# Two-layer hybrid trunk on one core: where raw weight blocks, W_down sums and the norm's ones-matmul stand

## The chip, the cores and the metric

The kernel runs on one core of a Trainium2 chip. The metric is the device time of one execution in microseconds; of several runs the median counts.

## The reference

The model is a trunk of two layers on an input of 1024 tokens by 1024 features, all in float32. Layer 0 mixes sparse attention with a Mamba-2 block, layer 1 is a short gated convolution, and behind each comes a SwiGLU network with a hidden width of 2816. The change touches what follows the attention:

```
def _short_conv_layer(x, norm_w, in_w, conv_w, out_w):
    h = _rmsnorm(x, norm_w) @ in_w
    gate_b, gate_c, v = _split(h, (SC_WIDTH, SC_WIDTH, SC_WIDTH))
    y = gate_b * _causal_dwconv(gate_c * v, conv_w)
    return x + y @ out_w

def _swiglu_ffn(x, norm_w, w_gate, w_up, w_down):
    h = _rmsnorm(x, norm_w)
    return x + (jax.nn.silu(h @ w_gate) * (h @ w_up)) @ w_down
```

The order is attention, FFN of layer 0 (here FFN0), short convolution (conv), FFN of layer 1 (FFN1), final norm.

## The kernel before

**Stages.** FFN0, conv and FFN1 are built alike. A stage normalises its input, multiplies it with the weights of the in-projection, combines the results elementwise, spills operands to DRAM, and then runs the out-projection (`out_products`). FFN0's and FFN1's in-projections have 22 units each, 11 pairs of a gate and an up block of 256 columns; conv's has 12, in 4 groups of c, v and b.

**A unit.** Every matrix product is made by a Strassen-Winograd scheme with 7 block products instead of 8. Each float32 operand is split into a high and a low part (`split`: ScalarE casts the high part, L176, VectorE subtracts it, L177), so a product of 4 blocks is 12 matmuls of 512 columns (`prod`, L1275 to L1277), and a full unit has 84. A unit's raw weights come as a pair of 512 KB tiles named `wr` (L1222). VectorE makes four sums of their quarters (L1198, L1201, tiles `s` and `wr`) and each block is split into a tile `wc`.

**Early products.** The norm of the two halves of the tokens isn't ready at the same time. Products 1 and 2 need the first half alone, so they are made ahead for the first 6 units of a stage (`early`). Their raw blocks (128x4x128, 256 KB, 12 in a stage) are loaded by `early_steps` (L1251) into the same two `wr` buffers that the pairs use; the pair tiles for the first unit come behind them. `norm_second` (L1492) normalises the second half: one matmul with a matrix of ones (L996) adds up the squares over the partitions, ScalarE takes the inverse root (L1004, L1005), VectorE multiplies (`scalar_tensor_tensor`, 8 of them, shown below as x<-x,c,sq). Before the change, it is called ahead of the first early product. In FFN1 it also holds `turn`, which transposes the residual on TensorE (L173) and stores it.

**W_down sums.** The out-projection's weights need sums of blocks too. They are made while the in-projection runs (`wsums`): for each of 11 pairs (4 groups in conv) four 256 KB loads into tiles `wd` (L1350, 4 buffers shared with other x tiles), four additions or subtractions, and four stores into a scratch tensor `d_wl` (L1340). In the kernel before, GpSimd (POOL) issues the loads and the stores and does the arithmetic. The out-projection then reads the sums back (L1389, tiles `lr`).

**What sets the order.** The program is written in one order, and a scheduler with a simulated timeline orders the instructions of each engine from it; buffers are handed out round robin by tag: `wr` has 2, `w` (the split weights) 8, `x` 4, `s` 32 and `t`, for temporaries, 42. A list of steps (`Steps`) makes the weights of a product 7 products ahead. SP's queue carries the weight loads, reads of operands, and stores of operands (`keep`, L1340 on SP).

Of the kernel before, what the change touches and what calls it, by code (L numbers as in the profile page):

```python
# [8 lines left out]
F32 = mybir.dt.float32  # L9
# [8 lines left out]
P = 128  # L18
# [3 lines left out]
HF = 512  # L22
# [81 lines left out]
class Trunk:  # L104
# [1108 lines left out]
    def unit_steps(self, src, prods, parts):  # L1213

        nc = self.nc
        st = {}

        def begin():
            st["r"] = []
            for i in range(2):  # L1220
                r = self.wp.tile([P, 4, 256], F32, name=self.uid("wr"), tag="wr", bufs=2)
                nc.sync.dma_start(r, src[i * HF:(i + 1) * HF].rearrange("(k p) m -> p k m", p=P))  # L1222
                st["r"].append(r)

        def step(i):
            if "r" not in st:
                begin()
            r0, r1 = st["r"]
            a11, a21, a12, a22 = r0[:, :, :P], r0[:, :, P:], r1[:, :, :P], r1[:, :, P:]
            if i == 6:  # L1230
                s3 = self.s(nm="s3")
                st["s3"] = s3.rearrange("p (k m) -> p k m", k=4)
                self.sub(st["s3"], a11, a21)
                self.add(a21, a21, a22)
                self.sub(a11, a21, a11)
            if i == 3:
                self.sub(a12, a12, a11)
            return self.wsplit({1: a11, 2: a12, 3: a12, 4: a22, 5: a21, 6: a11, 7: st.get("s3")}[i], 4)

        for i in prods:  # L1240
            if i in parts:
                self.st.note(parts[i])
            self.st.add(lambda i=i: step(i))

    def early_steps(self, src):

        nc = self.nc

        def step(i):
            r = self.wp.tile([P, 4, P], F32, name=self.uid("wr"), tag="wr", bufs=2)  # L1250
            nc.sync.dma_start(r, src[i * HF:(i + 1) * HF, :P].rearrange("(k p) m -> p k m", p=P))  # L1251
            return self.wsplit(r, 4)

        for i in range(2):
            self.st.add(lambda i=i: step(i))
# [31 lines left out]
        self.add(t, self.prod(H, 2), p1)  # L1287
        cons(0, 0, t)

    def early(self, H, cons):  # L1290

        out = []
        for n in range(self.EARLY_U):
            out.append(self.first_product(H))
            self.first_result(H, out[n], cons[n])
        return out

    def unit(self, H, cons, p1=None):
# [43 lines left out]
    def wsums(self, dn, k, nk, d, side):  # L1342

        nc = self.nc
        v = nc.gpsimd
        x = []
        for i in range(2):
            for c in range(2):
                t = self.x_(nm="wd")
                v.dma_start(t, dn[(2 * k + i) * P:(2 * k + i + 1) * P, c * HF:(c + 1) * HF])  # L1350
                x.append(t)
        if side == "L":
            a11, a21, a12, a22 = x
            self.add(a22, a21, a22, v)
            self.sub(a21, a11, a21, v)
            self.sub(a11, a22, a11, v)
            self.sub(a12, a12, a11, v)
            ops = {5: a22, 7: a21, 6: a11, 3: a12}
        else:
            b11, b12, b21, b22 = x  # L1360
            self.sub(b22, b22, b12, v)
            self.sub(b12, b12, b11, v)
            self.add(b11, b22, b11, v)
            self.sub(b21, b21, b11, v)
            ops = {7: b22, 5: b12, 6: b11, 4: b21}
        self.keep(ops, d, k, nk, v)

# [176 lines left out]
    def ffn_in(self, st, H, second):  # L1544
        nc = self.nc
        NP = st["NP"]
# [12 lines left out]
            return cons  # L1559

        cons = [f(p) for p in range(NP) for f in (gate, up)]
        second()
        p1 = self.early(H, cons[:self.EARLY_U])
        for p in range(NP):
            self.wsums(st["dn"], p, NP, st["d_w"], st["other"])
            for i in (2 * p, 2 * p + 1):
                self.unit(H, cons[i], p1[i] if i < len(p1) else None)
            s = S[p]
            if st["side"] == "R":
                ops = self.right(s[0, 0], s[0, 1], s[1, 0], s[1, 1])  # L1570
            else:
                ops = self.left(s[0, 0], s[1, 0], s[0, 1], s[1, 1])
            self.keep(ops, st["d_g"], p, NP)
            S[p] = None
            st["n"] += 1
# [99 lines left out]
    def conv_in(self, st, H, second):  # L1675
        nc = self.nc
# [30 lines left out]
            return cons  # L1707

        cons = [{"c": cc, "v": cv, "b": cb}[w](q) for w, q in self.CVB]
        second()  # L1710
        p1 = self.early(H, cons[:self.EARLY_U])
        for n, (w, q) in enumerate(self.CVB):
            if w == "c":
                self.wsums(st["dn"], q, 4, st["d_w"], "L")
            self.unit(H, cons[n], p1[n] if n < len(p1) else None)
            if w == "b":
                y = S[q][1]
                self.keep(self.right(y[0, 0], y[0, 1], y[1, 0], y[1, 1]), st["d_y"], q, 4)
                S[q] = None
                st["n"] += 1  # L1720
# [97 lines left out]
```

## Time and profile before

| | before |
|---|---|
| median of 3 runs | 2590.68 us (2585.49 to 2593.82) |
| the profiled execution | 2576.25 us, of it the span 2574.6 us |
| mean granted TensorE clock | 0.965 of full speed |
| TensorE busy | 2378.0 us, 92% |
| VectorE busy | 1996.0 us, 78% |
| ScalarE busy | 1152.8 us, 45% |
| GpSimd busy | 537.6 us, 21% |

TensorE is busy for nearly the whole span, so a stage is read by its gaps: a stretch of 50 us at full clock with no gap holds 222 or 223 matmuls of 512 columns, and a stretch with fewer has lost time to idleness or to a lower clock. The stages on TensorE run from 874 (FFN0's in-projection), 1343.6 (its out-projection), 1556.8 (conv), 1815.4 (conv's out-projection), 1933.7 (FFN1) and 2352 us (final out-projection) to 2562.5 us. The rows give start times from the span's beginning.

### The profile page before, as it was taken

How to read it: one execution, taken by the hardware profiler on the slowest of the kernel's cores; microseconds unless marked ns; L12 is line 12 of the kernel's file. 1: busy time of each engine (PE TensorE's matmuls, PEld its weight loads, DVE VectorE, ACT ScalarE, POOL GpSimd, SP SyncE). 2: the span in 40 equal slices, each digit the busy share in tenths (PEclk: the TensorE clock that was granted, in tenths of full speed). 3: DMA queues.
4: the chain of work that ended last, by engine and by line, in shares of the span. 5: the costliest groups of instructions: out<-in, count | busy, mean ns of one | idle time of the engine just before them, and what ended most of it. 6: DMA issues, size and time to landing. Idle time of an engine off the chain costs nothing.

```text
span 2574.6 us, 32108 instructions
## 1 busy us (share of the span) xinstructions
PE 2378.0 (92%) x10674; PEld 1924.4 (75%) x10674; DVE 1996.0 (78%) x3527; ACT 1152.8 (45%) x2215; POOL 537.6 (21%) x590
## 2 busy tenths in 40 slices
PE   6999989788988878999999989999979999999998
PEld 4788767566876656887887867788857888888886
DVE  4699978975587688988985676988778877776565
ACT  4655628784586441323233454223454333334443
POOL 1132221112102165556533220000200000001210
PEclk8999999889999989999999999999989999999999
DMA  4322346546753456667668753233642433336664
GB/s 116 79 69 89 116 147 190 156 139 183 239 150 115 135 177 232 229 214 238 211 217 277 237 189 106 74 119 103 233 160 91 147 95 106 107 107 225 215 206 163
DMA packets 290069, 411.97 MB, mean 160 GB/s; under 512 B 28210, under 2 KB 171760, under 8 KB 289904
## 3 DMA queue, kind: packets, MB, share of 16 engines
q1 hardware_dynamic: 251344, 282.50, 35.2%
q0 software_dynamic: 36256, 123.23, 14.0%
q10 hardware_dynamic: 2304, 4.20, 0.4%
q8 instruction: 84, 1.38, 0.2%
q14 instruction: 81, 0.66, 0.1%
HBM read 290.00 MB, written 117.21 MB: 158 GB/s over the span
## 4 chain that ended last, share of the span: by engine, by line
PE 41%; DVE 13%; DMA 6%; issue 3%; ACT 2%; POOL 1%; DVEq 0%; ACTq 0%; POOLq 0%; SPq 0%
PE mm L1275 5%; PE mm L1276 5%; PE mm L1277 5%; PE ps L1277 4%; PE ps L1275 4%; PE ps L1276 4%; DVE wc L177 3%; PE ps L1407 3%; PE ps L1408 3%; PE ps L1406 3%; PE mm L1406 2%; PE mm L1407 2%; PE mm L1408 2%; DMA wr<-in_l_w_up_dram 2%; DMA wr<-in_l_w_gate_dram 2%
## 5 line engine op out<-in xcount | busy, mean ns | idle before, releaser
L176 ACT CAST wc<-wr 128x512 fp32r<-128x512 f32 x336 | 202.8, 621 | 605.7 <-DVE wr L1201 348.8
L1275 PE MATMUL mm<-hh,wc 128*128 128x512 f32 x896 | 354.2, 395 | 11.9 <-ACT wc L176 7.3
L1276 PE MATMUL mm<-hl,wc 128*128 128x512 f32 x896 | 353.0, 394 | 0.0
L1277 PE MATMUL mm<-hh,wc 128*128 128x512 f32 x896 | 347.3, 390 | 0.0
L1275 PE MATMUL ps<-hh,wc 128*128 128x512 f32 x672 | 269.3, 401 | 36.0 <-ACT wc L176 35.9
L177 DVE TENSOR_TENSOR wc<-wr,wc 128x512 fp32r<-128x512 f32 x336 | 246.3, 740 | 52.0 <-ACT wc L176 49.0
L1277 PE MATMUL ps<-hh,wc 128*128 128x512 f32 x672 | 265.9, 396 | 1.7 <-DVE wc L177 1.7
L1276 PE MATMUL ps<-hl,wc 128*128 128x512 f32 x672 | 267.1, 397 | 0.0
L59 POOL TENSOR_TENSOR wl<-wr,wh 128x1024 fp32r<-128x1024 f32 (+1 forms) x55 | 135.7, 2470 | 487.2 <-ACT wh L58 464.1
L177 DVE TENSOR_TENSOR wc<-lr,wc 128x512 fp32r<-128x512 f32 x182 | 132.3, 731 | 122.0 <-ACT wc L176 121.9
L176 ACT CAST wc<-lr 128x512 fp32r<-128x512 f32 x182 | 112.9, 624 | 241.1 <-PE ps L1408 60.8
L167 PE MATMUL mm<-hh,wh 128*128 128x512 f32 (+1 forms) x496 | 198.0, 400 | 13.9 <-ACT hh L308 9.7
L1275 PEld LDWEIGHTS mm<-hh,wc 128*128 128x128 f32 x896 | 170.8, 191 | 52.1 <-ACT wc L176 10.5
L1276 PEld LDWEIGHTS mm<-hl,wc 128*128 128x128 f32 x896 | 171.0, 191 | 35.7 <-DVE hl L177 0.5
L168 PE MATMUL mm<-hl,wh 128*128 128x512 f32 (+1 forms) x496 | 196.7, 397 | 0.1
L169 PE MATMUL mm<-hh,wl 128*128 128x512 f32 (+1 forms) x496 | 195.7, 395 | 0.0
L1277 PEld LDWEIGHTS mm<-hh,wc 128*128 128x128 f32 x896 | 168.6, 188 | 35.5 <-DVE wc L177 0.4
L1275 PEld LDWEIGHTS ps<-hh,wc 128*128 128x128 f32 x672 | 129.5, 193 | 67.2 <-ACT wc L176 40.0
L1407 PE MATMUL ps<-rl,wc 128*128 128x512 f32 x416 | 163.8, 394 | 5.2 <-DVE rl L177 5.2
L1408 PE MATMUL ps<-rh,wc 128*128 128x512 f32 x416 | 162.8, 392 | 0.0
L1389 POOL DMA_DIRECT2D lr<-d_gl x42 | 29.0, 689 | 612.9 <-DVE wr L1201 446.0
L177 DVE TENSOR_TENSOR rl<-rr,rh 128x512 fp32r<-128x512 f32 x182 | 128.0, 706 | 30.9 <-ACT rh L176 30.4
(430 smaller groups left out, 5461.0 us busy)
## 6 DMA issues: line engine op xcount, KB each, us to landing
wr<-in_l_in_w_dram SPq DMA_DIRECT2D x54, 512.0 KB
wd<-in_l_w_down_dram POOLq DMA_DIRECT2D x88, 256.0 KB, 4.8
wr<-in_l_w_gate_dram SPq DMA_DIRECT2D x44, 512.0 KB
d_wl<-wd POOLq DMA_DIRECT2D x88, 256.0 KB, 2.6
wr<-in_l_w_up_dram SPq DMA_DIRECT2D x44, 512.0 KB
rr<-d_gl SPq DMA_DIRECT2D x77, 256.0 KB
lr<-d_gl POOLq DMA_DIRECT2D x35, 512.0 KB, 4.7
wr<-in_l_out_w_dram SPq DMA_DIRECT2D x24, 512.0 KB
```

The lines of the kernel that those rows point to most:

```text
L59: nc.gpsimd.tensor_tensor(lo, raw, f32(hi), op=ALU.subtract)
L167: self.nc.tensor.matmul(out, ah, bh, start=i == 0, stop=False)
L168: self.nc.tensor.matmul(out, ah, bl, start=False, stop=False)
L169: self.nc.tensor.matmul(out, al, bh, start=False, stop=i == n - 1)
L176: self.nc.scalar.copy(hi, src)
L177: (eng or self.nc.vector).tensor_tensor(lo, src, f32(hi), op=ALU.subtract)
L1275: self.nc.tensor.matmul(ps, wh[:, ks], h, start=k == 0, stop=False)
L1276: self.nc.tensor.matmul(ps, wh[:, ks], l, start=False, stop=False)
L1277: self.nc.tensor.matmul(ps, wl[:, ks], h, start=False, stop=k == n - 1)
L1406: self.nc.tensor.matmul(ps, wh[:, js], h, start=start, stop=False)
L1407: self.nc.tensor.matmul(ps, wh[:, js], l, start=False, stop=False)
L1408: self.nc.tensor.matmul(ps, wl[:, js], h, start=False, stop=stop)
```

## The change

Three things change.

- The early raw blocks are loaded into temporaries of tag `t`, each a tile of its own among 42, instead of the two `wr` buffers.
- `wsums` computes on VectorE. Its 104 loads go into SP's queue, and a scheduling order (no semaphore) puts each behind the latest load of unit weights; the stores stay in GpSimd's queue. The call moves from ahead of a pair's units to behind them, in conv from ahead of the c unit to behind the b unit.
- `second`, which calls `norm_second`, runs behind the first early unit instead of ahead of all six.

```
-                nc.sync.dma_start(r, src[i * HF:(i + 1) * HF].rearrange("(k p) m -> p k m", p=P))
+                self.wload = nc.sync.dma_start(r, src[i * HF:(i + 1) * HF].rearrange("(k p) m -> p k m", p=P))
...
-            r = self.wp.tile([P, 4, P], F32, name=self.uid("wr"), tag="wr", bufs=2)
-            nc.sync.dma_start(r, src[i * HF:(i + 1) * HF, :P].rearrange("(k p) m -> p k m", p=P))
-            return self.wsplit(r, 4)
+            r = self.t(nm="wr")
+            nc.sync.dma_start(r.rearrange("p (k m) -> p k m", k=4),
+                              src[i * HF:(i + 1) * HF, :P].rearrange("(k p) m -> p k m", p=P))
+            return self.wsplit(r)
...
-    def early(self, H, cons):
+    def early(self, H, cons, second):
         out = []
         for n in range(self.EARLY_U):
             out.append(self.first_product(H))
             self.first_result(H, out[n], cons[n])
+            if n == 0:
+                second()
...
-                v.dma_start(t, dn[(2 * k + i) * P:(2 * k + i + 1) * P, c * HF:(c + 1) * HF])
+                ld = nc.sync.dma_start(t, dn[(2 * k + i) * P:(2 * k + i + 1) * P, c * HF:(c + 1) * HF])
+                self.after(ld, self.wload)
...
-            self.add(a22, a21, a22, v)
+            self.add(a22, a21, a22)
...
-        second()
-        p1 = self.early(H, cons[:self.EARLY_U])
+        p1 = self.early(H, cons[:self.EARLY_U], second)
         for p in range(NP):
-            self.wsums(st["dn"], p, NP, st["d_w"], st["other"])
             for i in (2 * p, 2 * p + 1):
                 self.unit(H, cons[i], p1[i] if i < len(p1) else None)
+            self.wsums(st["dn"], p, NP, st["d_w"], st["other"])
...
-            if w == "c":
-                self.wsums(st["dn"], q, 4, st["d_w"], "L")
             self.unit(H, cons[n], p1[n] if n < len(p1) else None)
             if w == "b":
+                self.wsums(st["dn"], q, 4, st["d_w"], "L")
```

The other seven additions and subtractions of `wsums` change as the one shown.

In SP's queue at the end of the attention, the loads of the residual (`x`, behind L1160) stand ahead of the first early blocks before the change:

```order
L1160 DMA x_8482<-d_x_3256 128x512
L1160 DMA x_8494<-d_x_3256 128x512
L1160 DMA x_8547<-d_x_3256 128x512
L1160 DMA x_8566<-d_x_3256 128x512
L1251 DMA wr_8646<-in_l_w_up_dram 128x4x128
L1251 DMA wr_8651<-in_l_w_up_dram 128x4x128
L1251 DMA wr_8656<-in_l_w_gate_dram 128x4x128
L1251 DMA wr_8661<-in_l_w_gate_dram 128x4x128
```

Now the same queue has nine early blocks in a row there, and the eight residual loads come behind them:

```order
L1100 DMA rsb_8250<-d_rs 64x512 x2
L1251 DMA wr_8595<-in_l_w_gate_dram 128x4x128
L1251 DMA wr_8600<-in_l_w_gate_dram 128x4x128
L1251 DMA wr_8605<-in_l_w_up_dram 128x4x128
L1251 DMA wr_8610<-in_l_w_up_dram 128x4x128
L1251 DMA wr_8615<-in_l_w_gate_dram 128x4x128
L1251 DMA wr_8620<-in_l_w_gate_dram 128x4x128
L1251 DMA wr_8625<-in_l_w_up_dram 128x4x128
L1251 DMA wr_8630<-in_l_w_up_dram 128x4x128
L1251 DMA wr_8650<-in_l_w_gate_dram 128x4x128
L1160 DMA x_8422<-d_x_3256 128x512
L1160 DMA x_8440<-d_x_3256 128x512
```

Nine of the twelve early blocks of FFN0 have moved up past the residual loads.

Inside FFN0, SP's queue holds unit weights and stores of operands (`d_gl`) before the change:

```order
L1222 DMA wr_9165<-in_l_w_up_dram 128x4x256
L1222 DMA wr_9167<-in_l_w_up_dram 128x4x256
L1340 DMA d_gl_8360<-u_2069_9024 128x512
L1340 DMA d_gl_8360<-rt_9208 128x512
L1340 DMA d_gl_8360<-u_2066_9006 128x512
L1340 DMA d_gl_8360<-rt_9209 128x512
L1340 DMA d_gl_8360<-rt_9210 128x512
L1222 DMA wr_9296<-in_l_w_gate_dram 128x4x256
```

With the change, a group of four W_down loads stands behind the second pair of every gate and up pair:

```order
L1222 DMA wr_9149<-in_l_w_up_dram 128x4x256
L1222 DMA wr_9151<-in_l_w_up_dram 128x4x256
L1353 DMA wd_9192<-in_l_w_down_dram 128x512
L1353 DMA wd_9194<-in_l_w_down_dram 128x512
L1353 DMA wd_9196<-in_l_w_down_dram 128x512
L1353 DMA wd_9198<-in_l_w_down_dram 128x512
L1343 DMA d_gl_8360<-u_2065_9008 128x512
L1343 DMA d_gl_8360<-rt_9208 128x512
L1343 DMA d_gl_8360<-u_2062_8990 128x512
L1343 DMA d_gl_8360<-rt_9209 128x512
L1343 DMA d_gl_8360<-rt_9210 128x512
L1222 DMA wr_9280<-in_l_w_gate_dram 128x4x256
```

The next pair of unit weights has moved behind them, four places further back.

On VectorE, where a unit of FFN0 begins, the rows before hold the unit's weight sums (`s`, `wr`), the low parts (`wc`) and the running sums of products (`u`):

```order
L177 TENSOR_TENSOR wc_9276<-wr_9167,wc_9276 128x512
L1198 TENSOR_TENSOR u_2105_9238<-mm_9321,u_2105_9238 128x512
L1201 TENSOR_TENSOR s_2117_9300<-wr_9296 128x512
L1198 TENSOR_TENSOR u_2121_9339<-ps_9340,p_2009_8798 128x512
L1198 TENSOR_TENSOR wr_9296<-wr_9296,wr_9298 128x4x128
L1201 TENSOR_TENSOR wr_9296<-wr_9296 128x4x128
L1198 TENSOR_TENSOR u_2124_9357<-mm_9358,u_2121_9339 128x512
L1201 TENSOR_TENSOR wr_9298<-wr_9298,wr_9296 128x4x128
L177 TENSOR_TENSOR wc_9304<-wr_9296,wc_9304 128x512
```

With the change, sums on `wd` stand between them:

```order
L177 TENSOR_TENSOR wc_9260<-wr_9151,wc_9260 128x512
L1198 TENSOR_TENSOR c_2109_9275<-mm_9258,u_2104_9240 128x512
L1198 TENSOR_TENSOR u_2101_9222<-mm_9258,u_2101_9222 128x512
L1201 TENSOR_TENSOR wd_9192<-wd_9198,wd_9192 128x512
L1198 TENSOR_TENSOR u_2104_9240<-ps_9279,u_2104_9240 128x512
L1201 TENSOR_TENSOR s_2113_9284<-wr_9280 128x512
L1198 TENSOR_TENSOR u_2101_9222<-mm_9305,u_2101_9222 128x512
L1201 TENSOR_TENSOR wd_9196<-wd_9196,wd_9192 128x512
L1198 TENSOR_TENSOR u_2117_9323<-ps_9324,p_2009_8798 128x512
L1198 TENSOR_TENSOR wr_9280<-wr_9280,wr_9282 128x4x128
```

Two of a pair's four `wd` sums are seen here, ahead of the next unit's weight sums.

## Rows read from the trace of the kernel before

**Rows 1.** Busy time by stage (windows): FFN0, conv and FFN1 in-projection

```profile
core 0: us, PE busy (x) PEld busy (x) DVE busy (x) ACT busy (x) POOL busy (x), PEclk, DMA share, GB/s
874.00:1343.60 469.60, 436.83 (x1852) 355.24 (x1852) 406.19 (x538) 145.76 (x257) 247.36 (x298) 0.96 0.64 214
...
1933.70:2352.00 418.30, 412.03 (x1802) 340.14 (x1801) 333.31 (x524) 145.21 (x246) 3.57 (x5) 0.99 0.35 112
```

**Rows 2.** The same by 50 us

```profile
900.00:950.00 50.00, 34.71 (x125) 26.39 (x126) 46.97 (x64) 24.13 (x44) 35.36 (x36) 0.80 0.54 177
950.00:1000.00 50.00, 42.85 (x174) 34.32 (x173) 39.09 (x53) 10.57 (x19) 28.66 (x36) 0.93 0.68 223
1000.00:1050.00 50.00, 46.52 (x193) 37.52 (x193) 41.54 (x53) 9.57 (x17) 28.53 (x36) 0.93 0.68 229
...
1150.00:1200.00 50.00, 45.70 (x190) 37.22 (x189) 44.97 (x58) 12.92 (x23) 30.69 (x39) 0.93 0.72 235
1200.00:1250.00 50.00, 50.00 (x222) 41.41 (x221) 46.03 (x62) 14.64 (x26) 24.90 (x31) 1.00 0.65 223
...
1350.00:1400.00 50.00, 47.01 (x202) 37.18 (x201) 29.38 (x36) 18.63 (x35) 20.12 (x27) 1.00 0.89 307
```

**Rows 3.** TensorE's timeline: first instructions behind a gap (in brackets)

```profile
901.01 0.69 PE L1275 MATMUL mm<-hh,wc 128*128 128x512 f32 x1 [2.97 <-ACT p L1282]
...
922.78 0.79 PE L1275 MATMUL ps<-hh,wc 128*128 128x512 f32 x1 [8.98 <-ACT wc L176]
...
931.68 0.79 PE L1275 MATMUL mm<-hh,wc 128*128 128x512 f32 x1 [5.12 <-ACT wc L176]
...
1926.70 2.07 PE L996 MATMUL ps<-sq,c 128*128 128x512 f32 x2 [7.78 <-DVE sq L1198]
```

**Rows 4.** Windows from norm_second's start to the first unit's weights: FFN0, FFN1

```profile
889.87:931.50 41.63, 24.74 (x93) 18.98 (x91) 41.63 (x58) 20.52 (x37) 26.73 (x24) 0.80 0.44 140
1933.17:1965.54 32.37, 26.31 (x111) 20.89 (x109) 32.37 (x54) 20.33 (x38) 0.00 (x0) 0.90 0.17 62
```

**Rows 5.** VectorE by line and shape, 900 to 1350 us (GpSimd busy)

```profile
L177 DVE TENSOR_TENSOR wc<-wr,wc 128x512 fp32r<-128x512 f32 x121 | 99.7, 830 | 18.7 <-ACT wc L176 16.5
L1198 DVE TENSOR_TENSOR u<-mm,u 128x512 f32<-128x512 f32 x66 | 45.0, 681 | 1.4 <-PE mm L1277 1.3
L1201 DVE TENSOR_TENSOR wr<-wr,wr 128x512 f32<-128x512 f32 x22 | 22.5, 1023 | 0.3
```

**Rows 6.** The same, 1980 to 2350 us (GpSimd idle)

```profile
L177 DVE TENSOR_TENSOR wc<-wr,wc 128x512 fp32r<-128x512 f32 x114 | 78.2, 688 | 1.1 <-ACT wc L176 0.5
L1198 DVE TENSOR_TENSOR u<-mm,u 128x512 f32<-128x512 f32 x63 | 43.3, 687 | 26.3 <-PE mm L1277 25.9 <-DMA d_gl<-lt 0.3
```

**Rows 7.** GpSimd's lines, 900 to 1350 us

```profile
L1201 POOL TENSOR_TENSOR wd<-wd,wd 128x512 f32<-128x512 f32 x74 | 104.2, 1408 | 37.2 <-DMA wd<-in_l_w_down_dram 34.4
...
L1198 POOL TENSOR_TENSOR wd<-wd,wd 128x512 f32<-128x512 f32 x25 | 39.9, 1594 | 60.5 <-DMA wd<-in_l_w_down_dram 43.3 <-DMA wd<-in_l_out_w_dram 16.9
```

**Rows 8.** VectorE's timeline: first instruction on a new weight pair, FFN0 and FFN1

```profile
955.29 0.89 DVE L1201 TENSOR_TENSOR s<-wr 128x512 f32<-128x512 f32 x1 [4.42 <-DMA wr<-in_l_w_gate_dram]
...
1971.88 0.69 DVE L1201 TENSOR_TENSOR s<-wr 128x512 f32<-128x512 f32 x1 [2.02 <-DMA wr<-in_l_w_up_dram]
```

**Rows 9.** SP's waits, 860 to 1350 us: total us, times, longest

```profile
SPq L1251 <- DVE wc L177: 34.9, 10, 19.7
```

**Rows 10.** Windows: conv, FFN1's early units, the rest of FFN1

```profile
1650.00:1800.00 150.00, 149.75 (x661) 123.73 (x660) 133.61 (x227) 43.87 (x75) 1.45 (x2) 1.00 0.33 106
...
1980.00:2060.00 80.00, 80.00 (x355) 66.26 (x354) 69.89 (x114) 24.03 (x42) 0.00 (x0) 1.00 0.43 139
...
2060.00:2350.00 290.00, 290.00 (x1281) 240.23 (x1280) 217.16 (x335) 96.13 (x158) 3.57 (x5) 1.00 0.35 109
```

**Rows 11.** DMA issues of the page: KB each, us to landing

```profile
wd<-in_l_w_down_dram POOLq DMA_DIRECT2D x88, 256.0 KB, 4.8
d_wl<-wd POOLq DMA_DIRECT2D x88, 256.0 KB, 2.6
```

More of the change, by code (lines that the diff above doesn't have):

```diff
@@ L1353, in wsums @@
             a11, a21, a12, a22 = x
-            self.add(a22, a21, a22, v)
-            self.sub(a21, a11, a21, v)
-            self.sub(a11, a22, a11, v)
-            self.sub(a12, a12, a11, v)
+            self.add(a22, a21, a22)
+            self.sub(a21, a11, a21)
+            self.sub(a11, a22, a11)
+            self.sub(a12, a12, a11)
             ops = {5: a22, 7: a21, 6: a11, 3: a12}
@@ L1360, in wsums @@
             b11, b12, b21, b22 = x
[L1361 to L1364, printed above, removed]
+            self.sub(b22, b22, b12)
+            self.sub(b12, b12, b11)
+            self.add(b11, b22, b11)
+            self.sub(b21, b21, b11)
             ops = {7: b22, 5: b12, 6: b11, 4: b21}
@@ L1709, in conv_in @@
         cons = [{"c": cc, "v": cv, "b": cb}[w](q) for w, q in self.CVB]
-        second()
-        p1 = self.early(H, cons[:self.EARLY_U])
+        p1 = self.early(H, cons[:self.EARLY_U], second)
         for n, (w, q) in enumerate(self.CVB):
-            if w == "c":
-                self.wsums(st["dn"], q, 4, st["d_w"], "L")
             self.unit(H, cons[n], p1[n] if n < len(p1) else None)
             if w == "b":
+                self.wsums(st["dn"], q, 4, st["d_w"], "L")
                 y = S[q][1]
```

## The prediction

> **What bounds the kernel now.** The page says TensorE is busy for 92% of the span, so I first split the span into stages and 50-us windows and counted matmuls. A window with no loss, as 1200 to 1250 us, holds 222 [rows 2]; 0.225 us is then the price of one that is missing. FFN1's in-projection needs 418.3 us and FFN0's 469.6 us for the same 22 units, 1802 and 1852 matmul records [rows 1]: 50 more records explain 11 us, some 40 us are loss. It lies in four places. At the start (900 to 950 us) 97 matmuls are missing; from 950 to 1050 us 48 and 29; at 1150 to 1200 us 32; and 1350 to 1400 us, at the head of the out-projection, 20 [rows 2]. The timeline then says what TensorE waited for: the start has gaps of 2.97, 8.98 and 5.12 us, mostly for a split weight [rows 3].
>
> Behind the split weight stand two things. First VectorE: in FFN0 it is busy for 406.19 us with 538 instructions, in FFN1 for 333.31 us with 524 [rows 1]. The view by line tells why. With GpSimd at work, the subtraction that makes a low part takes 830 ns and a weight sum 1023 ns; with GpSimd idle the low part takes 688 ns. An addition with a PSUM operand takes 681 ns and 687 ns, so it doesn't suffer [rows 5, 6]. GpSimd works meanwhile on the W_down sums, 99 of 1.4 to 1.6 us, 144 us of the 450 [rows 7]. So the excess is due to GpSimd reading SBUF, and it is the whole of VectorE's surplus: 14 instructions more at 0.69 us are 10 us, the other 63 us are slowness.
>
> Second the weights: VectorE waited 4.42 us for a new pair in FFN0 and 2.02 us in FFN1 [rows 8], and the DMA engines are busy for 0.68 in the one stretch [rows 2], 0.43 in the other [rows 10], since GpSimd's loads run far ahead of need. SP itself waited 34.9 us in ten steps for a `wr` buffer before it could issue an early block [rows 9].
>
> The Trainium skill, "SBUF — State Buffer", section "Who interferes with whom", says a VectorE instruction with two SBUF inputs contends with a GpSimd instruction that reads SBUF, and that the loser blocks until the other ends. The trace agrees in kind (830 against 688 ns, PSUM-fed ones unchanged). By the page a GpSimd that only issues transfers would cost nothing there, which is what the sum below takes from the idle stretch.
>
> **The change part by part.** The sum is made against the profiled execution, 2576.25 us; the median of the runs, 2590.68 us, lies 14.4 us above it, and I add the change to the median.
>
> *Sums on VectorE.* It gains 104 instructions: 44 in FFN0, 16 in conv, 44 in FFN1. At the 0.69 us of an SBUF addition with GpSimd idle that is 30 us in FFN0 against 63 us of slowness that goes: VectorE ends 33 us freer there. Its own start-to-start spacing is less than the duration, 32.37 us for 54 instructions, 0.60 us each [rows 4], so 0.60 is the price in a stretch in which VectorE is the bound.
>
> 1. FFN0's start. From the first multiplication of norm_second (889.87 us) to the first unit's low part (931.50 us) VectorE runs without a pause, 58 instructions in 41.63 us, 0.72 each; FFN1's same stretch has 0.60 [rows 4]. In the new order it holds about as many, so 58 x 0.60 = 34.7: 7 us earlier; and the ten waits of SP for a buffer [rows 9] go, but the low parts of the last three early blocks now stand behind the multiplications on VectorE, so TensorE still idles in front of them. The ones-matmul stands some 23 matmuls (5 us) later on TensorE than it did, while the early products ahead of it start earlier, since their blocks are there: even. Taken: -8; bounds 0 and -17.1, the three gaps together [rows 3].
> 2. FFN0, 950 to 1050 us. 77 missing matmuls are 17.3 us. FFN1's early units, with VectorE unslowed, lose none (355 in 80 us) [rows 10]. But VectorE gets 12 sums there. Taken: three quarters, -13; bounds 0 and -17.3.
> 3. FFN0, 1150 to 1200 us. VectorE is busy for 44.97 of 50 us, GpSimd for 30.69 [rows 2], and a weight is late once. 32 matmuls, 7.2 us. Taken: -7; bounds 0 and -7.2.
> 4. Head of the out-projection, 1350 to 1400 us. The DMA share is 0.89 at 307 GB/s, since GpSimd already fetches conv's and FFN1's blocks. Those transfers move to conv and FFN1, which have shares of 0.33 and 0.35 [rows 10]. 20 matmuls, 4.5 us; taken -3, bounds 0 and -4.5.
> 5. FFN1's start. TensorE idles 7.78 us in front of the ones-matmul, waiting for the sums of squares [rows 3]. The new order puts two more early products (24 matmuls) between, and the out-projection's last matmuls some 40 places earlier, so the gap is filled. But the multiplications still start behind the ones-matmul, and what follows is VectorE's 32.37 us [rows 4], which is no shorter. Taken: -3; bounds 0 and -7.8.
> 6. Conv. GpSimd is idle there already, so VectorE has no slowness to lose: 133.61 of 150 us busy [rows 10], 16 sums more (9.6 us over 250 us). The norm's multiplications come at the same place. Taken: +1; bounds -2 and +4.
> 7. FFN1. In its early units VectorE is busy for 69.89 of 80 us [rows 10], by spacing 114 x 0.60 = 68.4; 12 sums more are 7.2 us and bring it to 95%. Beyond that, 217.16 of 290 us [rows 10] leave room for the other 32 sums (19 us). If the cover in the early units goes, each 0.6 us late is 0.6 us lost, at most 7.2 us. Taken: +4; bounds 0 and +8.
>
> *Loads in SP's queue.* 104 issues more. Each group of four stands behind the weight pair of a unit and waits for a `wd` buffer, which is free when the store of the previous group has landed, 2.6 us after its issue [rows 11]. Groups are a pair of units apart, 168 matmuls or 38 us, so the store should be long done; behind the waiting load stand operand stores and the next unit's weights, which themselves wait for VectorE to free `wr`. Cost taken: nothing, covered by that wait; without the cover see the slower case. In front of the first unit, nine early blocks now stand ahead of the eight residual loads, 2.4 MB, some 8 us at the 307 GB/s of [rows 2]; the last matmuls of the attention's output need the residuals only in their VectorE additions. Taken: nothing; at most +8.
>
> The Trainium skill, "DMA: Bandwidth & Descriptors", section "Issuing engines are not separate DMA queues", says transfers from any issuing engine interleave on the same 16 engines. By that rule a move from GpSimd's queue to SP's frees no bandwidth; with terms 2 and 4 at half for it, the sum would be -21. What the change alters is when they are issued, and [rows 2] show the rush.
>
> Sum: -8 -13 -7 -3 -3 +1 +4 = -29. 2576.25 becomes about 2547 us, and the median 2590.68 - 29 = 2562 us.
>
> **The rivals.**
>
> A. No gain that counts: the bound passes from GpSimd's interference to VectorE's own added work and to two `wr` buffers. The load of a pair can't start before VectorE has read the last one, so a unit's cycle stays load plus sums. For it: VectorE at 95% in term 7, and sums on `wd` that stand ahead of a new unit's weight sums. Against it: FFN1 has the same two buffers and loses nothing. Then term 1 is -4, 2 -4, 3 -3, 4 -2, 5 0, 6 +3, 7 +7: -3, 2588 us.
>
> B. All the gaps go: -17 -17 -7 -4.5 -7.8 -2 +0 = -55, 2535 us. For it: the slower granted clock behind each gap (0.80 and 0.93 in [rows 2]) comes back with it, and it is counted in the missing matmuls. Against it: the late low parts of term 1.
>
> C. Slower: SP's queue. If a group of `wd` loads waits for a store or lands after VectorE reaches its first sum, the queue of VectorE stands, and with it the low parts of the next unit. A load takes 4.8 us to land [rows 11], VectorE's wait for a pair is 2 to 4.4 us [rows 8]; four 256 KB loads right behind 1 MB of weights could make it 2 us more. On 26 groups that is +52 us of VectorE's time; with half of it hidden by what TensorE still has (it is ahead in the late units), +26, and +8 for the residual loads, against gains of 16 in terms 1 and 3: +18, 2609 us. It decides from about 1.5 us a group. Against it: VectorE waits for TensorE in FFN1 for 26.3 us on one line alone [rows 6], so it has slack.
>
> D. The early part does nothing: early products still wait, for split weights (8 buffers) or for VectorE, as before, and terms 1 and 5 are 0: -18, 2573 us.
>
> **How the numbers follow.** Forecast 0.50 (2562 us, its own range 2549 to 2574), D 0.11, A 0.13, B 0.12, C 0.14. A measurement of this kernel can tell about 0.3%, 8 us, from no change. Faster: forecast, D and B, with a little of A, 0.75; the same: most of A and a little of C, 0.12; slower: C, 0.13. The range reaches from B to above A, 2533 to 2600 us, which leaves out C's middle and the far end of B.
>
> **What would show it.** Right: VectorE's low parts at about 690 ns in FFN0; 950 to 1050 us, shifted by the gain, with over 210 matmuls in each 50; no gap of 7 us ahead of the ones-matmul of FFN1; a GpSimd with no arithmetic in these stages; FFN0's in-projection 25 to 30 us shorter. Wrong: waits of VectorE for `wd`, or of TensorE in FFN1 for split weights, of over 8 us together; an SP queue that waits for stores of `wd`; late residuals at the end of the attention.

## The result, and the profile after

| | before | after |
|---|---|---|
| median, four runs each | 2589.66 us (2585.49 to 2593.82) | 2554.69 us (2550.72 to 2557.34) |
| ratio | | 0.9875, 95% interval 0.9839 to 0.9911 |
| the profiled execution | 2576.25 us, span 2574.6 us | 2550.72 us, span 2549.0 us |
| TensorE / VectorE / GpSimd busy | 2378.0 / 1996.0 / 537.6 us | 2371.5 / 1970.4 / 332.4 us |

The forecast was -29 us and 2562 us; the medians lie 35 us apart, and 2554.69 us is inside the range. To see where the time went I took seven marks from the two traces, each the start of a matmul but the last. The attention, whose matmuls no run here alters, ended at 851.75 us in the profile of before and at 857.47 us in that of after (the start of its last matmul, L1116), so each mark is counted from there.

| mark, us behind the attention's last matmul | before | after | step's gain |
|---|---|---|---|
| FFN0's sixth unit done (504th product matmul) | 179.7 | 153.6 | -26.1 |
| FFN0's in-projection done | 491.5 | 458.2 | -7.2 |
| half of its out-projection | 601.1 | 563.2 | -4.6 |
| conv's sixth unit done | 849.0 | 806.8 | -4.3 |
| conv's in-projection done | 963.2 | 923.0 | +2.0 |
| FFN1's sixth unit done | 1195.5 | 1164.3 | +9.0 |
| end of the span | 1722.8 | 1691.5 | -0.1 |

The sum is -31.3 us. FFN0 gives more than all of it, and the way from conv's out-projection to FFN1 takes 9 us back. In windows of the profile after (columns as in [rows 1]), FFN0's in-projection, then the 50-us stretches that answer to [rows 2], shifted by the gain where the stage is:

```profile
876.90:1315.90 439.00, 427.90 (x1863) 351.15 (x1862) 364.92 (x587) 153.00 (x260) 29.48 (x53) 0.98 0.48 159
900.00:950.00 50.00, 39.01 (x152) 30.14 (x151) 45.83 (x77) 24.43 (x44) 0.00 (x0) 0.86 0.19 58
950.00:1000.00 50.00, 49.93 (x220) 41.00 (x220) 42.91 (x71) 12.73 (x23) 2.70 (x5) 1.00 0.59 195
1000.00:1050.00 50.00, 49.97 (x221) 41.07 (x220) 41.73 (x69) 16.29 (x29) 4.85 (x9) 1.00 0.55 185
1150.00:1200.00 50.00, 50.00 (x222) 41.41 (x221) 40.83 (x65) 15.33 (x25) 4.32 (x8) 1.00 0.44 149
1320.00:1370.00 50.00, 50.00 (x222) 41.41 (x221) 26.64 (x42) 23.16 (x42) 6.97 (x10) 1.00 0.77 258
```

The 77, 32 and 20 matmuls that were missing in [rows 2] are back but for three. What is left is the start: 152 of 222. VectorE is busy for 364.92 us where it was 406.19 us [rows 1], with 49 instructions more.

VectorE's lines between 900 and 1315 us, as [rows 5], and GpSimd's stores, the largest of what is left on its line view (860 to 1350 us), as [rows 7]:

```profile
L177 DVE TENSOR_TENSOR wc<-wr,wc 128x512 fp32r<-128x512 f32 x123 | 83.7, 688 | 10.7 <-ACT wc L176 9.9
L1198 DVE TENSOR_TENSOR u<-mm,u 128x512 f32<-128x512 f32 x65 | 44.6, 686 | 9.2 <-PE mm L1278 9.1
L1201 DVE TENSOR_TENSOR wd<-wd,wd 128x512 f32<-128x512 f32 x33 | 22.6, 686 | 0.0
```

```profile
L1343 POOL DMA_DIRECT2D d_wl<-wd x44 | 23.7, 540 | 386.5 <-DVE wd L1198 341.2 <-DVE wd L1201 45.3
```

A low part takes 688 ns instead of 830 ns, and VectorE now waits for TensorE (9.2 us of idleness in front of u<-mm, 1.4 us before): it is no longer the bound. GpSimd makes none of the sums.

The two stretches behind norm_second, as [rows 4]:

```profile
896.74:930.32 33.58, 22.79 (x82) 16.94 (x80) 33.58 (x56) 19.22 (x35) 0.00 (x0) 0.80 0.04 16
1907.39:1940.00 32.61, 22.67 (x86) 17.17 (x84) 32.61 (x54) 20.82 (x39) 0.00 (x0) 0.79 0.29 97
```

And TensorE's timeline, as [rows 3]: FFN0's start, FFN1's ones-matmul and start.

```profile
911.18 0.79 PE L1276 MATMUL ps<-hh,wc 128*128 128x512 f32 x1 [6.00 <-ACT wc L176]
...
919.04 0.79 PE L1278 MATMUL ps<-hh,wc 128*128 128x512 f32 x1 [3.50 <-DVE wc L177]
...
1901.85 1.02 PE L996 MATMUL ps<-sq,c 128*128 128x512 f32 x2
...
1921.83 0.80 PE L1276 MATMUL ps<-hh,wc 128*128 128x512 f32 x1 [5.37 <-ACT wc L176]
```

The 7.78 us in front of FFN1's ones-matmul are gone, and FFN0's start has two larger gaps instead of three.

### The profile page after: what moved, and what is told of

Same layout as the page of the kernel before. It is cut to its first block, busy times and chain, and to the rows that moved or that the text cites. A ratio compares the mean times of both kernels' runs of the same rounds, so it can differ in the third digit from the quotient of the medians.

```text
span 2549.0 us, 32290 instructions
## 1 busy us (share of the span) xinstructions
PE 2371.5 (93%) x10674; PEld 1922.4 (75%) x10674; DVE 1970.4 (77%) x3631; ACT 1156.1 (45%) x2221; POOL 332.4 (13%) x382
## 4 chain that ended last, share of the span: by engine, by line
PE 61%; DVE 11%; DMA 4%; ACT 3%; issue 3%; SPq 0%; POOL 0%; DVEq 0%; ACTq 0%; POOLq 0%
PE mm L1276 7%; PE mm L1277 7%; PE mm L1278 7%; PE ps L1278 5%; PE ps L1277 5%; PE ps L1276 5%; PE ps L1411 4%; PE ps L1412 3%; PE ps L1410 3%; PE mm L1410 2%; PE mm L1411 2%; PE mm L1412 2%; DVE hl L177 2%; DMA xt<-in_x_dram 1%; DVE wc L177 1%
## 5 line engine op out<-in xcount | busy, mean ns | idle before, releaser
L177 DVE TENSOR_TENSOR wc<-wr,wc 128x512 fp32r<-128x512 f32 x336 | 227.1, 689 | 27.6 <-ACT wc L176 25.9
L177 DVE TENSOR_TENSOR wc<-lr,wc 128x512 fp32r<-128x512 f32 x182 | 124.7, 690 | 122.2 <-ACT wc L176 122.0
L1276 PEld LDWEIGHTS ps<-hh,wc 128*128 128x128 f32 x672 | 128.2, 191 | 50.7 <-ACT wc L176 24.1
L1278 PEld LDWEIGHTS ps<-hh,wc 128*128 128x128 f32 x672 | 127.9, 190 | 42.2 <-DVE wc L177 15.5
```

Of the source, the lines that this page charges most:

```text
L177: (eng or self.nc.vector).tensor_tensor(lo, src, f32(hi), op=ALU.subtract)
L1276: self.nc.tensor.matmul(ps, wh[:, ks], h, start=k == 0, stop=False)
L1278: self.nc.tensor.matmul(ps, wl[:, ks], h, start=False, stop=k == n - 1)
```

## The experiments

The runs came in four groups, each timed beside the kernel before on its own chip, where that had a median of 2576.89 us (first to fourth run), 2581.01 us (fifth to eighth), 2575.86 us (ninth to eleventh) and 2583.39 us (twelfth). So ratios are compared, and for stages the marks of the traces: "FFN0" is the time from the attention's last matmul to the end of FFN0's in-projection (491.5 us before, 458.2 us after), "rest" that to the end (1722.8 and 1691.5 us).

| run | ratio (95% interval) | FFN0, us | rest, us |
|---|---|---|---|
| early tiles alone | 1.0013 (0.9993 to 1.0034) | 501.6 | 1721.5 |
| sums and paced loads alone | 0.9906 (0.9884 to 0.9928) | 456.2 | 1696.1 |
| later norm_second alone | 1.0049 (1.0030 to 1.0068) | 499.3 | 1735.1 |
| after without the later norm_second | 0.9915 (0.9892 to 0.9937) | 462.0 | 1696.9 |
| arithmetic on VectorE, loads as before | 1.0002 (0.9980 to 1.0024) | 488.4 | 1728.9 |
| paced loads, arithmetic on GpSimd | 0.9888 (0.9850 to 0.9926) | 466.4 | 1703.5 |
| after again | 0.9880 (0.9846 to 0.9914) | 457.6 | 1697.5 |
| after, SiLU behind the norm | 0.9880 (0.9845 to 0.9914) | 456.1 | 1693.5 |
| after and 88 loads | 0.9914 (0.9887 to 0.9941) | 461.5 | 1697.1 |
| after and 99 GpSimd additions | 1.0079 (1.0050 to 1.0107) | 502.3 | 1747.2 |
| after, conv's sums behind c | 0.9862 (0.9834 to 0.9890) | 457.4 | 1685.3 |
| sums alone, conv's behind c | 0.9857 (0.9833 to 0.9881) | 454.8 | 1684.6 |

**The three parts one by one.** Theory 1 was the prediction's: the gain is GpSimd's arithmetic that leaves SBUF. Theory 2 came from the trace after: with norm_second behind the first early unit, a SiLU comes between the two steps of the inverse root on ScalarE, and table loads of 1.28 us with it. The first run is the kernel before with

```
-            r = self.wp.tile([P, 4, P], F32, name=self.uid("wr"), tag="wr", bufs=2)
...
+            r = self.t(nm="wr")
...
```

> The kernel before with the first part alone: early raw blocks in temporaries. Theory 1 (the gain is GpSimd's arithmetic leaving SBUF, the early tiles matter little because the low parts of the early blocks still stand on a slowed VectorE): -5 to 0 us against before. Rival (early blocks that arrive early pull the start of each stage ahead): -12 us or more, with FFN0's first gaps (2.97, 8.98, 5.12 us) gone.

Measured: 1.0013, no difference. FFN0 even takes 10 us longer, and the stages behind it give that back. The second is all hunks of the change that have to do with `wsums`, and nothing else:

```
+                ld = nc.sync.dma_start(t, dn[(2 * k + i) * P:(2 * k + i + 1) * P, c * HF:(c + 1) * HF])
+                self.after(ld, self.wload)
...
-            self.add(a22, a21, a22, v)
+            self.add(a22, a21, a22)
...
```

> The kernel before with the second part alone: W_down sums on VectorE, loads behind the weights in SP's queue, call behind the units. Theory 1: most of the gain, -22 to -30 us, low parts at about 690 ns in FFN0, no window under 215 matmuls between 960 and 1300 us. Rival (the early tiles carry the gain, VectorE is the bound either way): -10 us or less.

Measured: 0.9906, -24 us, and FFN0 at 456.2 us, as short as with all parts. The third:

```
             self.first_result(H, out[n], cons[n])
+            if n == 0:
+                second()
```

> The kernel before with the third part alone: norm_second behind the first early unit. Theory 2 (it costs: the ones-matmul queues behind early products on TensorE, and a SiLU comes between the two steps of the inverse root on ScalarE, 3 table loads of 1.28 us each in FFN0 and in FFN1): +5 to +12 us against before. Rival (it fills the 7.78 us gap ahead of FFN1's ones-matmul): -3 to -8 us.

Measured: 1.0049, 13 us slower, theory 2's sign and a little over its size. In FFN0 TensorE stands for 16.21 us at one place, where [rows 3] had 8.98:

```profile
929.52 0.79 PE L1275 MATMUL ps<-hh,wc 128*128 128x512 f32 x1 [16.21 <-ACT wc L176]
...
938.02 0.79 PE L1275 MATMUL mm<-hh,wc 128*128 128x512 f32 x1 [4.72 <-ACT wc L176]
```

The fourth is after with the third part taken back (`second()` ahead of `early`).

> The kernel after without the third part: norm_second ahead of all early products, as before. Theory 2: faster than after by 5 to 12 us, -40 to -47 us against before, the first multiplication of FFN0's second norm about 7 us earlier than in after (896.74 us). Rival: slower than after by 3 to 8 us, -27 to -32 us against before, with the gap ahead of FFN1's ones-matmul back.

Measured: 0.9915. It is not faster than after, so theory 2 falls here; as for the rival, the ratios (0.9915, and 0.9875 and 0.9880 for after) overlap in their intervals. FFN0 is 4 us longer than in after (462.0 against 458.2 and 457.6 us). TensorE's timeline shows a place for that: with early tiles and an early norm, TensorE stands for 12.85 us in front of an early product, for a split weight.

```profile
893.86 0.79 PE L1276 MATMUL mm<-hh,wc 128*128 128x512 f32 x1 [12.85 <-ACT wc L176]
```

**What in the second part is the gain.** It does two things: it moves the arithmetic to VectorE, and it holds the loads behind the unit weights, so that the sums are spread over the stages instead of running ahead. `v` is the engine that does the arithmetic, GpSimd where it is named and VectorE where it is left out. The fifth run is the kernel before with `v` left out in the eight additions and subtractions and nothing else.

```
-            self.add(a22, a21, a22, v)
+            self.add(a22, a21, a22)
```

> The kernel before with nothing but the arithmetic of the W_down sums moved to VectorE; loads and stores stay in GpSimd's queue and the call stays ahead of the units. Theory 1 (the interference of GpSimd's arithmetic is the main price): low parts at about 690 ns in FFN0 and most of the second part's gain, -15 to -25 us. Rival (the gain is the pacing of the loads behind the weights): -8 to +5 us, since the loads still run ahead on GpSimd's queue and VectorE may stand at sums whose loads are late.

The rival was right: 1.0002. The sixth keeps the second run's loads and the place of the call, and puts `v` back in the eight.

```
-            self.add(a22, a21, a22)
+            self.add(a22, a21, a22, v)
```

> The kernel before with the loads of the W_down sums paced in SP's queue and the call behind the units, but the arithmetic left on GpSimd. Theory 1: low parts still at 780 ns or more wherever sums run, now in conv and FFN1 too; -5 to -12 us, for the weights that land sooner in FFN0 alone. Rival (pacing is the gain): -18 us or more.

Again the rival: 0.9888, as much as after, although GpSimd does the sums. VectorE's lines between 900 and 1350 us in these two, the fifth run first, and GpSimd's in the sixth, with the number of sums (`wd`) on either:

```profile
L177 DVE TENSOR_TENSOR wc<-wr,wc 128x512 fp32r<-128x512 f32 x122 | 82.0, 682 | 18.0 <-ACT wc L176 17.5
L1201 DVE TENSOR_TENSOR wd<-wd,wd 128x512 f32<-128x512 f32 x75 | 51.2, 683 | 11.3 <-DMA wd<-in_l_w_down_dram 11.2
L1198 DVE TENSOR_TENSOR u<-mm,u 128x512 f32<-128x512 f32 x65 | 44.2, 680 | 0.0
L1198 DVE TENSOR_TENSOR wd<-wd,wd 128x512 f32<-128x512 f32 x25 | 17.1, 685 | 9.6 <-DMA wd<-in_l_w_down_dram 5.3 <-DMA wd<-in_l_out_w_dram 4.3
```

```profile
L177 DVE TENSOR_TENSOR wc<-wr,wc 128x512 fp32r<-128x512 f32 x123 | 102.6, 838 | 8.0 <-ACT wc L176 7.2
L1198 DVE TENSOR_TENSOR u<-mm,u 128x512 f32<-128x512 f32 x66 | 45.1, 683 | 15.6 <-PE mm L1277 15.3
```

```profile
L1201 POOL TENSOR_TENSOR wd<-wd,wd 128x512 f32<-128x512 f32 x33 | 46.1, 1396 | 1.3
L1198 POOL TENSOR_TENSOR wd<-wd,wd 128x512 f32<-128x512 f32 x11 | 16.9, 1534 | 332.1 <-DMA wd<-in_l_w_down_dram 248.9 <-ACT wc L176 83.2
```

In the fifth, low parts are fast (682 ns), but 100 sums stand on VectorE in FFN0, the 44 of FFN0 and those of later stages, and wait there for their loads besides (20.8 us); VectorE never waits for TensorE (0.0 in front of u<-mm). In the sixth, low parts are slow (838 ns), but only 44 sums are made in FFN0, and VectorE does wait for TensorE (15.3 us). So neither the slow nor the fast low parts decide. What the two runs differ in is how many sums are made while FFN0 runs, and whether their loads run ahead. Three things make up the pacing, SP's queue, the order behind the weights and the later call, and no run takes them apart.

**After again, and the table loads.**

> The kernel after, on the chip of the other runs of this group. From its first measurement 0.9875 of before; by the parts measured one by one (-24, +3, +13 us, and -22 us for the first two together) the sum would be only -9 us: theory 3 says that early tiles and the later norm work together (the norm may stand behind early products only if their blocks are there), so about -27 to -32 us; a plain sum of the parts says -9 us.

Measured: 0.9880, 29 us, so the first figure holds, and the plain sum falls: the third part costs 13 us alone and nothing that can be measured beside the other two. Theory 3 says that it is the early tiles that take this cost away. That isn't shown: the paced sums may do it, since no run has them with the later norm and without the tiles. In the eighth run the SiLU waits for the end of the inverse root on ScalarE:

```
-            self.first_result(H, out[n], cons[n])
             if n == 0:
-                second()
+                self.first_result(H, out[n], lambda *r: (second(), cons[0](*r)))
+            else:
+                self.first_result(H, out[n], cons[n])
...
-                nc.scalar.activation(t, t, AF.Silu)
+                self.after(nc.scalar.activation(t, t, AF.Silu), self.rexp)
```

> The kernel after with the first early unit's SiLU ordered behind the inverse root on ScalarE, so the table loads between its two steps go. Theory 2: 3 table loads of 1.28 us less in FFN0 and in FFN1, of which the one between the two steps and some waiting lie on the way to the norm's multiplications: 2 to 3 us each, -3 to -6 us against after. Rival (the ones-matmul's place on TensorE sets the time, the tables are hidden): within 1 us of after.

The table loads went, as ScalarE's timelines show (after, then the eighth run):

```profile
889.43 1.28 ACT L1004 ACT_TABLE_LOAD   x1
894.07 0.69 ACT L1004 ACTIVATE sq<-ps,c 128x512 f32<-128x512 f32 x1 [3.36 <-PE ps L996]
894.78 1.28 ACT L1005 ACT_TABLE_LOAD   x1
896.07 0.63 ACT L1005 ACTIVATE sq<-sq 128x512 f32<-128x512 f32 x1
```

```profile
892.66 0.69 ACT L1004 ACTIVATE sq<-ps,c 128x512 f32<-128x512 f32 x1 [6.60 <-PE ps L996]
893.38 0.63 ACT L1005 ACTIVATE sq<-sq 128x512 f32<-128x512 f32 x1
```

The time didn't change (0.9880): the inverse root waits for the ones-matmul on TensorE in both, and one table load of 1.28 us is all that lay on the path in FFN0. The rival fits; FFN0, at 456.1 us against 457.6 and 458.2, leaves room for the 1.28 us, and a gain of 3 us on the whole would be too small for these intervals.

**Transfers or arithmetic.** Sums that run ahead on GpSimd bring both transfers and slow VectorE instructions into FFN0. Two runs add one of them to after. In the ninth and tenth, the tiles `dm` come out of the temporaries (40 instead of 42).

```
+            if st["side"] == "R":
+                for i in range(8):
+                    t = self.t(nm="dm", tag="dm")
+                    r = (2 * p + i % 2) * P
+                    ld = nc.gpsimd.dma_start(t, st["dn"][r:r + P, (i // 2 % 2) * HF:(i // 2 % 2 + 1) * HF])
+                    self.after(ld, self.wload)
```

> The kernel after with 88 additional loads of 256 KB that nothing reads, 8 to a pair of units, issued from GpSimd's queue in FFN0 alone (their two tiles are taken from the 42 temporaries); no arithmetic is added. Theory 4 (transfers ahead of need delay the weights, and that was the price before): VectorE's waits for weight tiles in FFN0 go from some 17 back to 30 us, FFN0's in-projection loses 8 to 18 us, +8 to +18 us against after. Theory 1 (interference of GpSimd's arithmetic): within 3 us of after.

```
+            if st["side"] == "R":
+                for i in range(9):
+                    self.after(nc.gpsimd.tensor_tensor(self.dm[1], self.dm[0], self.dm[0], op=ALU.add), self.wload)
```

> The kernel after with 99 additional GpSimd additions on tiles of their own, 9 to a pair of units, in FFN0 alone (as many as it did there before; tiles from the temporaries as in the run beside it); no transfers are added, and nothing reads the sums. Theory 4: low parts back at some 830 ns, but the time within 5 us of after, since VectorE has room between the weights. Theory 1: +10 to +20 us against after.

The windows from 900 to 1350 us (columns as in [rows 1]) of before, after, the ninth and the tenth run, then of the fifth and the sixth:

```profile
900.00:1350.00 450.00, 419.78 (x1781) 342.47 (x1782) 394.60 (x516) 139.20 (x247) 248.48 (x298) 0.95 0.65 217
```

```profile
900.00:1350.00 450.00, 438.90 (x1914) 360.60 (x1913) 370.12 (x595) 155.33 (x270) 31.73 (x56) 0.98 0.52 174
```

```profile
900.00:1350.00 450.00, 436.08 (x1901) 358.18 (x1900) 364.12 (x588) 148.32 (x263) 77.38 (x139) 0.98 0.66 221
```

```profile
900.00:1350.00 450.00, 405.08 (x1718) 324.51 (x1717) 402.48 (x540) 126.80 (x227) 141.95 (x139) 0.97 0.42 145
```

```profile
900.00:1350.00 450.00, 417.12 (x1761) 334.19 (x1760) 369.52 (x604) 132.83 (x238) 111.61 (x204) 0.97 0.64 217
```

```profile
900.00:1350.00 450.00, 435.20 (x1880) 357.73 (x1879) 371.43 (x541) 151.54 (x259) 92.11 (x98) 0.98 0.51 173
```

The ninth run brings the DMA share back to that of before (0.66 against 0.65), VectorE's waits for weight tiles rise from 17.9 to 27.6 us (sums over the four groups of its waits), and FFN0 loses 3.3 us (461.5 against 458.2); the ratio is 0.9914 against 0.9880, 9 us, but the intervals overlap. In FFN0's trace theory 4 falls in its size (8 to 18 us), and transfers are a small part; the times alone don't exclude it. The tenth has less traffic than any (0.42), and FFN0 loses 44 us, more than all it had won; the whole, at 1.0079, is slower than before. Its low parts take 859 ns:

```profile
L177 DVE TENSOR_TENSOR wc<-wr,wc 128x512 fp32r<-128x512 f32 x123 | 104.6, 859 | 12.3 <-ACT wc L176 11.2
L1198 DVE TENSOR_TENSOR u<-mm,u 128x512 f32<-128x512 f32 x63 | 42.9, 680 | 0.0
```

VectorE has now 44 sums of its own and the slowing by 99 of GpSimd's, and is the bound (0.0 us of waiting for TensorE).

I hold one account for the cause: in FFN0 VectorE has room for some 44 W_down sums and not for 99, and a sum costs it about the same wherever it is made. The tenth run bears out the first half: with 99 additions on GpSimd beside VectorE's 44, all that FFN0 had won is lost. The second half rests on estimates. By [rows 1, 7] GpSimd's 99 cost VectorE 63 us, 0.64 us each; on VectorE one takes 0.69 us (22.6 us for 33). Before is then 63 us and 491 us in FFN0; the tenth, 63 + 30 = 93 us and 502 us; after, 30 us and 458 us; the sixth, 44 x 0.64 = 28 us and 466 us. The sixth is 8 us longer than after with as much work (its profile is of the slowest of its six executions); VectorE's busy time is nearly equal in the two, 371.43 and 370.12 us.

The fifth run doesn't fit by prices alone: 100 x 0.69 = 69 us should make it longer than before, and it is 3 us shorter. VectorE is busy for 369.52 us there, 25 us less than before and no more than in after. It stands instead, for 20.8 us in front of sums whose loads haven't landed and for 36.3 us in front of weight pairs (the sums over the groups of its waits are 31.5 us before and 17.9 us in after). So on VectorE part of the price of 100 sums in FFN0 is waiting, and no run separates that from the work.

**The way from conv to FFN1.** In after, TensorE stops at the head of conv's out-projection, where before it didn't: 176 matmuls in the first 50 us against 219 before. The windows of before and after, and TensorE's gaps in after:

```profile
1815.20:1865.20 50.00, 50.00 (x219) 40.52 (x218) 36.66 (x60) 23.53 (x42) 10.77 (x17) 1.00 0.78 266
```

```profile
1780.70:1830.70 50.00, 42.26 (x176) 33.59 (x176) 33.74 (x55) 18.70 (x33) 7.85 (x12) 0.97 0.70 247
```

```profile
1794.49 2.07 PE L1410 MATMUL ps<-rh,wc 128*128 128x512 f32 x4 [5.43 <-ACT rh L176]
1799.64 1.20 PE L1410 MATMUL mm<-rh,wc 128*128 128x512 f32 x4 [0.77 <-ACT rh L176]
1806.63 1.20 PE L1410 MATMUL mm<-rh,wc 128*128 128x512 f32 x4 [1.23 <-ACT rh L176]
```

SP's queue gives one reason: an operand (`rr`) of the out-projection is read behind stores of conv's results (`d_y<-cacc`), which wait for VectorE.

```profile
1784.07 3.92 SPq L1343 DMA_DIRECT2D d_y<-cacc  x3
1788.94 0.32 SPq L1395 DMA_DIRECT2D rr<-d_y  x1
```

ScalarE, which splits the operands, shows a second: it stood first for a W_down sum that is read back (`lr<-d_wo`), and behind that hardly at all for `rr`. The two came within a microsecond of each other.

```profile
1793.05 0.62 ACT L176 CAST wc<-lr 128x512 fp32r<-128x512 f32 x1 [4.00 <-DMA lr<-d_wo]
1793.82 0.62 ACT L176 CAST rh<-rr 128x512 fp32r<-128x512 f32 x1 [0.16 <-DMA rr<-d_y]
```

The eleventh run moves conv's sums one step up:

```
-            if w == "b":
+            if w == "c":
                 self.wsums(st["dn"], q, 4, st["d_w"], "L")
+            if w == "b":
```

> The kernel after with conv's W_down sums behind the c unit of a group instead of its b unit. Theory 5 (the last group's sums and conv's last products compete on VectorE, so the operand stores for the out-projection come late, and TensorE's gaps of 5.43, 0.77 and 1.23 us at conv's out-projection follow): these gaps go, -4 to -9 us against after. Rival (the gaps come from the W_down blocks on GpSimd's queue): no change within 2 us.

SP's queue and the 50 us from the head of the out-projection there:

```profile
1778.42 2.12 SPq L1343 DMA_DIRECT2D d_y<-cacc  x2
1782.80 0.32 SPq L1395 DMA_DIRECT2D rr<-d_y  x1
```

```profile
1780.00:1830.00 50.00, 49.68 (x216) 39.62 (x214) 35.96 (x60) 22.99 (x42) 11.32 (x18) 1.00 0.75 259
```

The gaps are gone, and the rest falls from 1691.5 and 1697.5 us (two profiles of after) to 1685.3 us, -6 to -12 us. From the end of conv's in-projection to FFN1's sixth unit it takes 232.1 us, as before (232.2); the eight profiles with paced sums behind b (after, the second, the fourth and the sixth to tenth run) have 240.1 to 243.9 us. The ratio is 0.9862; its interval overlaps that of after, so a gain over after is shown by the traces, not by the times. Theory 5 holds in that the late sums make the gaps. Whether by the operands or by the sums read back isn't shown, since the edit moves both; the rival's "no change" leaves that out. The last run drops the first and the third part: the second run with this edit.

> The second part of the change alone (sums on VectorE, loads paced in SP's queue), with conv's sums behind the c unit; no early tiles, norm_second where it was. Theory 6 (the first and the third part together are worth nothing): 0.986 of before, as the run with all parts and conv's sums behind c. Rival (together they are worth some 5 us): 0.988 to 0.990. In either case conv's out-projection has no gap of over 1 us in its first 20 us.

Measured: 0.9857, 2542.79 us. Theory 6 holds within the intervals (some 6 us either way), and FFN0 (454.8 against 457.5 us) and the rest (1684.6 against 1685.3 us) agree: nothing is lost without the early tiles and the later norm. With the eleventh it is the fastest version measured here, and it has one of the three parts.

## Why the prediction was right, and where it wasn't

The time, the sign and the stage were right. Point by point:

1. *FFN0's start*, -8: VectorE's stretch took 33.58 us for 56 instructions (0.60 each, as forecast), and from the attention's end to the first unit's low part it is 72.8 us instead of 79.8: -7. The start of the norm's multiplications moved by 1 us, so "even" was right. But what was credited to early loads there isn't so: with the sums alone FFN0 is as short.
2. *950 to 1050 us*, -13: with term 1 -21; measured -26.1 to the sixth unit, 19 of it behind term 1's 7. Under-sized: nearly all 77 matmuls came back, not three quarters.
3. *1150 to 1200 us*, -7: measured -7.2.
4. *Head of the out-projection*, -3: measured -4.6, and another -4.3 up to conv's sixth unit that was on no list. It is there by the out-projection's last matmul (719.6 and 677.4 us); what made it isn't shown.
5. *FFN1's start*, -3: the 7.78 us gap went and nothing was won. In the eleventh run, where conv's gaps are out of the way, FFN1's sixth unit is done as long behind conv's in-projection as before (the two marks moved by -37.4 and -37.6 us), and in the twelfth, with the norm where it was, it takes 232.3 us against the eleventh's 232.1. The prediction itself said that the multiplications still start behind the ones-matmul and that what follows is no shorter; by that the term was 0.
6. *Conv*, +1: the term that failed. +2.0 in conv's in-projection, and 9.0 us more up to FFN1's sixth unit. I counted VectorE's time over the stage, 133.61 of 150 us [rows 10], and not its last microseconds, where the last group's sums push conv's results, their stores in SP's queue and the reads behind them. That is rival C's shape (stores and reads in one queue) at a place that I didn't look at; the sums read back come late there too.
7. *FFN1's early units*, +4: 352 matmuls in 80 us against 355 [rows 10], some 0.7 us; in-projection from there without loss. Over-sized: the cover held.

So the sum, -29 against -31.3 in the traces, is near partly by luck: terms 2, 3 and 4, the unlisted 4.3 us and term 7 gave some 15 us more than forecast, terms 1, 5 and 6 some 13 us less.

The prediction also named signs of being wrong, and two of them came. SP's `wd` loads waited for stores of `wd`, 13.5 us in nine waits behind the attention. VectorE's waits for `wd`, with TensorE's in FFN1, were to stay under 8 us; from 860 us to the end of after VectorE's alone are 28.3 us:

```profile
DVE wd L1201 <- DMA wd<-in_l_w_down_dram: 14.5, 9, 2.4
DVE wd L1198 <- DMA wd<-in_l_w_down_dram: 13.8, 9, 2.7
```

That is 1.1 us for each of 26 groups, under the 1.5 us from which rival C was to decide. FFN0 became shorter all the same; what these waits cost no run shows.

The cause was half right. "The excess is due to GpSimd reading SBUF" holds as far as GpSimd's additions go: the tenth run brings the slow low parts and 44 us with them, while the ninth's transfers weigh 3 us in FFN0. No run tells their reads from their writes. The slowness was under-sized: VectorE's busy time in FFN0 fell by 41.3 us with 44 sums more, so at 0.69 us a sum some 71 us of slowness went, not 63. But the prediction gave the gain to the move of the arithmetic ("30 us in FFN0 against 63 us of slowness that goes"), and that comparison hides what makes it: 99 sums in FFN0 against 44. The fifth run, arithmetic moved and nothing paced, gains nothing; the sixth, paced and not moved, gains all that can be measured. The pacing, which the prediction costed at nothing, is the change. The Trainium skill ("SBUF — State Buffer", section "Who interferes with whom") says that a VectorE instruction with two SBUF inputs contends with a GpSimd instruction that reads SBUF. The traces agree in what slows: low parts take 838 and 859 ns with GpSimd's additions beside them, 682 to 690 ns without.

Of the rivals, A lost (FFN1 lost no more than 0.7 us). B's terms for FFN0, -41, weren't reached: -33.3, nearer the forecast's -28. C's waits came, and its shape cost time at conv's end. D was right that the early part does nothing: 1.0013 by itself, and the twelfth run loses nothing without it; but its total, -18, is refuted, since term 1's stretch shortened without the early tiles.

## What to carry to other kernels

When an engine that runs ahead slows another, ask how much of its work falls into the stage that is bound, before asking which engine should do it: spreading 99 sums over three stages was worth some 24 us, moving them between engines nothing that could be measured. A stage's mean load hides its last microseconds; read what VectorE does just before a stage ends, and which stores and reads queue behind that. Parts of a change can cost alone and be free together (13 us for the later norm alone, nothing measurable beside the other two parts), so take them apart before keeping them all.

## What was not expected of the hardware

An unchanged stage took 851 to 858 us from one profiled execution to another, so stages had to be counted from its end; a difference of 6 us in a span isn't yet one of the change. And the price of interference is about the price of the work: by the two estimates above 0.64 to 0.72 us of VectorE's time (63 or 71 us for 99) for each of GpSimd's additions, which take 1.4 to 1.6 us there, against 0.69 us for doing it itself.
